# Token norms of a DeltaNet layer: squares by wide activations and sums by one-column matmuls in place of per-token accumulating activations

## The chip, the cores and the metric

The kernel runs on one core of one Trainium2 chip. The metric is device microseconds (us) of one execution. A core has TensorE (PE; the trace shows its weight loads apart, as PEld), VectorE (DVE), ScalarE (ACT), GpSimd (POOL) and SyncE (SP), whose queue here issues every DMA. Matmul results land in PSUM, which this kernel uses as eight banks, each a tile of 128 partitions by 512 words; the other tiles lie in SBUF.

## The reference, cut to what matters

One layer of a token mixer (a Fourier branch and a bidirectional gated DeltaNet branch) followed by a ConvFFN, for 1024 tokens and 256 context tokens of width 1024, in float32. The change touches three norms, each over the 128 channels of one head, per token:

```python
def l2norm(x):
    return x * lax.rsqrt(jnp.sum(x * x, axis=-1, keepdims=True) + L2_EPS)

qkv = jax.nn.silu(dwconv1d(p[..., OFF_Q:OFF_Z], conv_qkv)).astype(jnp.float32)
q, k, v = [a.reshape(b, t, DN_HEADS, DN_HEAD_DIM) for a in jnp.split(qkv, 3, axis=-1)]
q = l2norm(q) * (DN_HEAD_DIM ** -0.5)
k = l2norm(k)
...
o = (rms_norm(o_dn, dn_norm) * jax.nn.silu(zh)).astype(z.dtype).reshape(b, t, DN_WIDTH)
```

There are 8 heads. k is needed for 1280 tokens (1024 and the 256 of context), q and the delta output o for 1024. So the sums of squares are 8 x (10 + 8 + 8) = 208 blocks of 128 tokens by 128 channels.

## The kernel before, in words

**Layout.** A head's k, q, v and o stand with the 128 channels on the partitions and the tokens along the free axis (`xs` tiles of 128 x 1280, `qT` and `oo` of 128 x 1024). A norm per token is therefore a sum over partitions. The kernel wants it with the tokens on the partitions: one column of 128 values for each block of 128 tokens.

**How the order of the work is made.** `layer` (from line 488) only records operations. `Program.schedule` (line 351) is a list planner: it prices every operation with `cost` (line 247), takes the dependences from tiles and buffers, gives each operation a rank (the length of the priced path that hangs on it, plus a bonus) and builds one queue for each engine, which the engine then runs in order. PE is one such queue: a matmul that waits holds all that stand behind it. A PSUM bank counts as one whole in the dependences (line 305): a write to any part of it waits for the earlier reads of it by other engines. A buffer that several tiles share is handed on when the last user of the tile before is done (`gates`, line 323).

**The stages.** After the conditioning vector and the context projections, `project_kv` (line 942) makes k and v of a head: projection on PE with float32r matmuls in three terms (high and low halves), convolution taps on ACT and DVE, a SiLU (`silu_of_half`, line 754: tanh on ACT in pieces of 512 tokens into a tile of the ring `th`, which has two buffers, then one DVE operation), then ten blocks turned over by PE transposes in three groups (`o` in 8, 0, 4), copied out of PSUM by ACT (`tk`) and stored to `knd`. These transposes serve the stored token-major k and v; for k, ACT then squares each turned block in PSUM with an accumulating activation that leaves the 128 sums in one column of `ssq` (lines 965 to 967). Heads 0 to 3 take their banks from X0, X1, Y0, Y1, heads 4 to 7 from pm and pd in turn. `rk`, the inverse norm of k, is needed early: `coefs` (line 779) turns it into the factors of `decay_products`.

`kq_head` (line 1080) projects q and calls `query_norms`, which calls `squares` (line 762): eight transposes of `qT` in two groups of four into bank pd, eight accumulating squares. `scan_head` (line 1100) runs the recurrence over eight chunks in both directions, stores the output `oo`, and calls `squares` on it with the banks Y0 and Y1. Both results meet in `rs` (line 1126), the power on POOL, one small transpose and a store to `rsd`. `rsd` is read only in `gated` (line 1324), after all heads.

The main loop (line 1227) goes over ten stages (two context groups `c0`, `c1` and eight heads `x0` to `x7`): the scan of a stage, the block inversion (on DVE, with DMA round trips through DRAM) and merge of the next one, the q projection of the one after. `sides` fills in projections that nobody waits for soon (k and v of heads 4 to 7, the gates z and g). In the trace this delta part lies from about 100 to 1000 us. After it come the output projections, and from about 1300 us the ConvFFN.

**Prices that the planner uses** for the operations here: a transpose of 128 x 128 109 ns, a float32 matmul `n * 4 / 2.4 + 5` ns, where n is the larger of the columns of the moving and of the stationary operand (218 ns at 128, line 257), an activation `51 or 93 + 0.833 n` ns and 93 more with an accumulator (line 269).

Of the kernel before, what the change touches and what calls it, by code (L numbers as in the profile page):

```python
# [9 lines left out]
F32 = mybir.dt.float32  # L10
F32R = mybir.dt.float32r
AF = mybir.ActivationFunctionType
ALU = mybir.AluOpType
# [3 lines left out]
P = 128  # L17
# [8 lines left out]
EPS = 1e-6  # L26
AHEAD = 50
HALF = 512
# [160 lines left out]
class Program:  # L189
# [8 lines left out]
    def pool(self, name, bufs=1, space=None, side="left"):  # L198
        p = Pool(self, name, bufs, space, side)
        if space is None:  # L200
            self.events.append((True, p))
        return p
# [44 lines left out]
    def cost(self, eng, method, args, kw):  # L247
        out = args[0] if args else kw["out"]
        shape = out.shape
        n = math.prod(shape[1:])  # L250
        ins = [x for x in list(args[1:]) + list(kw.values()) if isinstance(x, View)]
        psum = any(v.slot.space == PSUM for v in ins)
        if eng == "PE":
            if method == "transpose":
                return max(53, args[1].shape[0] * 2 / 2.4 + 2)
            rhs, m = args[2], math.prod(args[1].shape[1:])
            n = max(math.prod(rhs.shape[1:]), m)
            if rhs.shape[0] <= 64 and m <= 64:
                return 34 if n <= 32 else 80
            return n / 2.4 + 3 if rhs.dtype == F32R and n >= 256 else n * 4 / 2.4 + 5  # L260
        if eng == "DVE":
            if method == "reciprocal":
                return 65 + 6.3 * n
            ptr = any(v.shape[-1] == 1 and v.arr.size <= P for v in ins) and method in ("tensor_scalar", "scalar_tensor_tensor")
            fast = method in ("tensor_copy", "tensor_scalar") and not psum and out.slot.space != PSUM
            return 66 + n / (1.92 if fast else 0.96) + (61 if ptr else 0)
        if eng == "ACT":
            aps = any(isinstance(kw.get(x), View) for x in ("scale", "bias", "accum_out"))
            return (51 if psum else 93) + n * 0.833 + (93 if aps else 0)
        if eng == "POOL":  # L270
            if method == "memset":
                return 36 + 0.83 * n
            if kw.get("op") == ALU.pow:
                return 300 + 165 * n
            if method == "tensor_copy":
                return 119 + 3.33 * n
            if method == "affine_select":
                return 1060
            return 140 + 2.12 * n
        run = 1  # L280
        view = out if isinstance(out, View) else args[1]
        if isinstance(view, View):
            a_ = view.arr
            for d in range(a_.ndim - 1, -1, -1):
                if a_.shape[d] > 1 and a_.strides[d] != run:
                    break
                run *= a_.shape[d]
        total = math.prod(shape) * 4
        return max(60.0, total / 359.0 * (1 if run * 4 >= 512 else 2))
# [192 lines left out]
def body(tc, a, out):  # L482
    prog = Program(tc)
    layer(prog, a, out)
    prog.run()


def layer(prog, a, out):
    te, ve, se, po, sp = (prog.eng[n] for n in ("PE", "DVE", "ACT", "POOL", "SP"))
    pool, close = prog.pool, prog.close  # L490

    const = pool("const", bufs=1)
# [4 lines left out]
    def cload(name, shape=None, src=None):  # L497
        src = a[name] if src is None else src
        t = const.tile(list(shape or src.shape), F32, name=f"c_{name}")
        sp.dma_start(t, src)  # L500
        return t

    def ps(tag, shape, name):
        return psum.tile(shape, F32, tag=tag, name=name, bufs=PPB if tag == "pp" else 1)
# [3 lines left out]
    def bank(shape, name):  # L508
        rota[1] += 1
        return ps(rota[0][rota[1] % len(rota[0])], shape, name)  # L510
# [4 lines left out]
    ident = cload("ident", src=a["cst"][:, 0:128])  # L515
# [3 lines left out]
    ones = const.tile([P, 2], F32, name="ones")  # L519
# [19 lines left out]
    def weights(src, name, eng=None, tags=("h", "l"), pl=None):  # L539
        return [halves(src[:, o:o + HALF], pl or wst, tags, f"{name}{o}", eng) for o in range(0, src.shape[-1], HALF)]  # L540

    def product(pt, wl, rhs, nk=KT):
        n = 0
        for k in range(nk):
            h, l = rhs(k)
            wh, wlo = wl[k // 4]
            ks = slice((k % 4) * P, (k % 4 + 1) * P)
            for w_, r_ in ((wh, h), (wh, l), (wlo, h)):
                te.matmul(pt, w_[:, ks], r_, start=n == 0, stop=n == 3 * nk - 1)
                n += 1  # L550

    def split(h, l, src, eng_h=None, eng_l=None):
        if eng_h is se:
            se.activation(h, src, AF.Copy)
        else:
# [7 lines left out]
    bufs = {"CL": 2, "xs": 2, "qT": 2, "kT": 2, "F": 4, "LT": 2, "th": 2,  # L563
            "N": 4, "qh": 2, "S": 4, "R": 2, "vt": 3}
# [4 lines left out]
    def dt(tag, name, shape=(P, T), dtype=F32):  # L569
        return dp.tile(list(shape), dtype, tag=tag, name=name, bufs=bufs.get(tag, 1))  # L570
# [4 lines left out]
    th = dt("vt", "tanh_c", (P, KT, 2))  # L575
# [48 lines left out]
    for k in range(KT):  # L624
# [4 lines left out]
        for half in range(1, 2):  # L629
            parts = halves(a["w_ada"][k * P:(k + 1) * P, half * 1024:(half + 1) * 1024], hx, ("H", "L"),  # L630
                           f"ada{k}{half}", (ve, po)[k % 2])
            for j in range(2):
                for i, w_ in enumerate(parts):
                    te.matmul(rows[half * 2 + j], s4[:, k, :], w_[:, j * HALF:(j + 1) * HALF], start=k + i == 0,
                              stop=k == KT - 1 and i == 1)
    prog.bonus = 0.0
    pm_ = ps("pm", [P, 16, 4], "modp")
    for q in range(4):
        n = (2, 4)[q // 2]
# [32 lines left out]
    NCH = 10  # L672
# [75 lines left out]
    def conv_taps(pt, acc, w3):  # L748
        n = acc.shape[-1]
        se.activation(acc, pt[:, 0:n], AF.Identity, scale=w3[:, 1:2])  # L750
        ve.scalar_tensor_tensor(acc[:, 1:n], pt[:, 0:n - 1], w3[:, 0:1], acc[:, 1:n], op0=ALU.mult, op1=ALU.add)
        ve.scalar_tensor_tensor(acc[:, 0:n - 1], pt[:, 1:n], w3[:, 2:3], acc[:, 0:n - 1], op0=ALU.mult, op1=ALU.add)

    def silu_of_half(acc, name):
        n = acc.shape[-1]
        for o in range(0, n, HALF):
# [2 lines left out]
            se.activation(th_, part, AF.Tanh)  # L759
            ve.scalar_tensor_tensor(part, th_, 1.0, part, op0=ALU.add, op1=ALU.mult)  # L760

    def squares(src, name, tags):
        ssq = const.tile([P, 8], F32, tag="ssq", name=f"ssq_{name}", bufs=3)
        for g in range(2):
            pt = ps(tags[g], [P, 4, P], f"sq_{name}{g}")
            for i in range(4):
                u = g * 4 + i
                te.transpose(pt[:, i, :], src[:, u * P:(u + 1) * P], ident)
            for i in range(4):
                se.activation(pt[:, i, :], pt[:, i, :], AF.Square, accum_out=ssq[:, g * 4 + i:g * 4 + i + 1])  # L770
        return ssq

    def query_norms(src, name):
        qn = const.tile([P, 8], F32, tag="qn", name=f"qn_{name}", bufs=3)
# [164 lines left out]
    rk_of = const.tile([P, NH, NCH], F32, name="rk_of")  # L939
    turn = [0]  # L940

    def project_kv(w, h):
        kv = "kv"[w]
        wl = weights((wi_k, wi_v)[w](h), f"{kv}{h}")
        dst = xsp.tile([P, T + TC], F32, tag="xs", name=f"xs{kv}{h}")
        w3 = convw[:, (w + 1) * 8 + h, :]
        pt = bank([P, HALF], f"pc{w}_{h}")
        product(pt[:, 0:TC], wl, hc)
        conv_taps(pt, dst[:, T:T + TC], w3)
        proj_taps(wl, dst, w3, f"x{kv}_{h}")  # L950
        silu_of_half(dst, f"th{kv}{h}")
        if w == 0:
            sp.dma_start(kvd[h], dst)
            ssq = const.tile([P, NCH], F32, tag="ssq", name=f"ssq_k{h}", bufs=3)
        for o in (8, 0, 4):
            n = min(4, NCH - o)
            turn[0] += 1
            tags = XY if h < 4 else ("pm", "pd")
            pt = ps(tags[turn[0] % len(tags)], [P, 4, P], f"tt{kv}{h}_{o}")
            for i in range(n):  # L960
                te.transpose(pt[:, i, :], dst[:, (o + i) * P:(o + i + 1) * P], ident)
            tk = dp.tile([P, 4, P], F32, tag="tk", name=f"tk{kv}{h}_{o}", bufs=2)
            se.activation(tk[:, 0:n, :], pt[:, 0:n, :], AF.Copy)
            sp.dma_start(knd[w, h, :, o:o + n, :], tk[:, 0:n, :])
            if w == 0:
                for i in range(n):
                    se.activation(pt[:, i, :], pt[:, i, :], AF.Square, accum_out=ssq[:, o + i:o + i + 1])
        if w == 0:
            rk = rk_of[:, h, :]
            ve.tensor_scalar(rk, ssq, EPS, None, op0=ALU.add)  # L970
            po.tensor_tensor(rk, rk, mhalf[:, 0:NCH], op=ALU.pow)

    def load_tokens(w, name, src):
# [242 lines left out]
    for h in range(4):  # L1216
        project_kv(0, h)
# [36 lines left out]
    for g4 in range(NF):  # L1254
# [18 lines left out]
        for e in range(2):  # L1273
            pt = ps(("pd", "pm")[e], [P, 4, P], f"dft{g4}{e}")
            for i in range(4):
                te.matmul(pt[:, i, :], quad[:, e, i // 2, (i % 2) * P:(i % 2 + 1) * P], csd[:, e * P:(e + 1) * P],
                          start=True, stop=True)
            se.activation(gh[:, e], pt, AF.Copy)
        pt = ps("pd", [1, P], f"mid{g4}")
# [4 lines left out]
        for e in (1, 0):  # L1284
            pt = ps(("pm", "pd")[e], [P, 2, QT], f"dfp{g4}{e}")
            for odd in range(2):
                more = e == 0 and odd == 0
                for i in range(2):
                    te.matmul(pt[:, odd, :], gh[:, e, odd * 2 + i, :], waves[e][:, odd, i, :], start=i == 0,
                              stop=i == 1 and not more)  # L1290
# [12 lines left out]
    pt = ps("pd", [P, NF], "dftn")  # L1303
# [196 lines left out]
    for ts in ((0,), (1,), (2,), (3,), (4,), (5, 6, 7)):  # L1500
# [20 lines left out]
        g = ts[-1] // 4  # L1521
        prog.bonus = BON * (1 - g)
        for k in (0, 4, 1, 5, 2, 6, 3, 7) if g == 0 else (4, 5, 6, 7, 0, 1, 2, 3):
            pt = transposed(xn[-4:], k, f"h2{g}", ("pd", "pm")[k % 2])
# [273 lines left out]
```

## Time and profile before

| | |
|---|---|
| runs | 2049.98, 2051.59, 2053.32 us, median 2051.59 |
| profiled execution | 2047.95 us, of which the span of the program's instructions is 2046.2 us |
| granted TensorE clock, mean | 0.979 |
| PE busy | 1953.0 us (95%), 11470 instructions |
| weight loads (PEld) | 1570.9 us (77%) |
| DVE / ACT / POOL busy | 1363.1 / 858.1 / 564.0 us |
| ACT squares with accumulator, blocks of 128 x 128 in PSUM | 208, each followed by a readout of the accumulator |

How to read it: a group's row gives the operation, the shapes (stationary operand as rows*columns for PE, then the moving or source tile), the count, then the busy time in us, the mean of one in ns, and the idle time of the engine before them with what ended it. A timeline row gives start and length in us of a run of like instructions, their count, and in brackets the idle time before the first. PE and PEld records overlap each other; the pitch (start to start) and not the mean length is what one more instruction costs. All instructions carry line 349, the place where the recorded operations are issued, so the names of tiles (p for PSUM, m for SBUF, d for DRAM) and the shapes tell them apart.

### The profile page before, as it was taken

How to read it: one execution, taken by the hardware profiler on the slowest of the kernel's cores; microseconds unless marked ns; L12 is line 12 of the kernel's file. 1: busy time of each engine (PE TensorE's matmuls, PEld its weight loads, DVE VectorE, ACT ScalarE, POOL GpSimd, SP SyncE). 2: the span in 40 equal slices, each digit the busy share in tenths (PEclk: the TensorE clock that was granted, in tenths of full speed). 3: DMA queues.
4: the chain of work that ended last, by engine and by line, in shares of the span. 5: the costliest groups of instructions: out<-in, count | busy, mean ns of one | idle time of the engine just before them, and what ended most of it. 6: DMA issues, size and time to landing. Idle time of an engine off the chain costs nothing.

```text
span 2046.2 us, 31495 instructions
## 1 busy us (share of the span) xinstructions
PE 1953.0 (95%) x11470; PEld 1570.9 (77%) x11470; DVE 1363.1 (67%) x2848; ACT 858.1 (42%) x2088; POOL 564.0 (28%) x573
## 2 busy tenths in 40 slices
PE   8989999899999999999999999979999999999998
PEld 3868888787777788778776778857878888878886
DVE  5648767667677577673655485479988889882132
ACT  5575354555354453632431032454444444532121
POOL 3110121101112220210221000257878888600000
PEclk9989999899999999999999999999999999999999
DMA  7153324344451543441778562312222222453231
GB/s 298 52 187 92 105 88 132 117 145 128 113 149 52 149 150 92 118 114 51 223 234 289 181 221 102 114 52 78 95 75 80 83 83 86 167 181 100 77 126 52
DMA packets 180637, 257.52 MB, mean 126 GB/s; under 512 B 75921, under 2 KB 97522, under 8 KB 180482
## 3 DMA queue, kind: packets, MB, share of 16 engines
q1 hardware_dynamic: 180482, 255.51, 39.0%
q8 instruction: 90, 1.47, 0.3%
q14 instruction: 65, 0.53, 0.1%
HBM read 194.52 MB, written 60.94 MB: 125 GB/s over the span
## 4 chain that ended last, share of the span: by engine, by line
PE 71%; DVE 14%; DMA 5%; ACT 5%; issue 2%; POOL 1%; SPq 0%; DVEq 0%; POOLq 0%; ACTq 0%
PE p L349 71%; DVE m L349 11%; ACT m L349 4%; DMA m<-d 3%; DVE p L349 3%; DMA d<-m 2%; ACT p L349 1%; POOL m L349 1%; DMA m<-in_w_ada_dram 1%; SPq L349 0%; DMA m<-in_wu_dram 0%; ACT L349 0%; DVEq L1787 0%; POOLq L1787 0%; DVEq L349 0%
## 5 line engine op out<-in xcount | busy, mean ns | idle before, releaser
L349 PE MATMUL p<-m,m 128*128 128x512 f32 (+7 forms) x11310 | 1937.8, 338 | 75.7 <-ACT m L349 31.6
L349 PEld LDWEIGHTS p<-m,m 128*128 128x128 f32 (+4 forms) x11310 | 1551.2, 174 | 452.6 <-ACT m L349 62.4
L349 DVE TENSOR_TENSOR m<-m,m 128x512 fp32r<-128x512 f32 (+27 forms) x1096 | 557.4, 523 | 253.4 <-ACT m L349 222.8
L349 ACT ACTIVATE m<-m 128x512 fp32r<-128x512 f32 (+8 forms) x649 | 411.3, 652 | 613.5 <-DMA m<-d 161.0
L349 POOL TENSOR_TENSOR m<-m,m 128x512 fp32r<-128x512 f32 (+5 forms) x338 | 449.5, 1353 | 782.6 <-DVE m L349 625.1
L349 ACT ACTIVATE m<-p 128x512 f32<-128x512 f32 (+5 forms) x510 | 221.1, 448 | 329.3 <-PE p L349 286.0
L349 DVE SCALAR_TENSOR_TENSOR m<-p,m,m 128x128 f32<-128x128 f32 (+4 forms) x488 | 203.1, 452 | 92.3 <-ACT m L349 40.9
L349 DVE SCALAR_TENSOR_TENSOR p<-m,m,p 128x512 f32<-128x512 f32 x352 | 240.1, 749 | 2.7 <-ACT p L349 0.4
L349 ACT ACTIVATE m<-p,m 128x128 f32<-128x128 f32 (+2 forms) x240 | 115.7, 495 | 184.3 <-PE p L349 179.5
L349 POOL MEMSET m<- 128x1024 f32 (+7 forms) x79 | 35.7, 460 | 381.7 <-PE p L349 224.0
L349 POOL COPY m<-m 32x256 f32<-32x256 f32 (+2 forms) x136 | 60.3, 447 | 211.5 <-DMA m<-d 173.7
L349 DVE SCALAR_TENSOR_TENSOR m<-m,m 128x512 f32<-128x512 f32 (+5 forms) x119 | 65.7, 558 | 28.6 <-ACT m L349 16.3
L349 DVE COPY m<-p 32x256 f32<-32x256 f32 (+11 forms) x116 | 42.1, 368 | 62.5 <-PE p L349 32.8
L349 DVE TENSOR_TENSOR m<-p,m 128x512 f32<-128x512 f32 (+4 forms) x91 | 57.8, 645 | 30.5 <-PE p L349 29.1
L349 DVE SCALAR_TENSOR_TENSOR m<-m,m,m 128x1024 f32<-128x1024 f32 (+2 forms) x68 | 59.6, 878 | 26.0 <-DMA m<-in_w_ada_dram 25.6
L349 DVE TENSOR_TENSOR m<-m,p 128x128 f32<-128x128 f32 (+3 forms) x117 | 53.4, 458 | 29.6 <-PE p L349 28.8
L349 ACT ACTIVATE p<-p 128x128 f32<-128x128 f32 x208 | 55.4, 266 | 25.6 <-PE p L349 23.6
L349 DVE SCALAR_TENSOR_TENSOR m<-m,p 128x512 f32<-128x512 f32 x76 | 50.7, 682 | 13.9 <-ACT m L349 7.7
L349 DVE SCALAR_TENSOR_TENSOR m<-m,m,p 128x128 f32<-128x128 f32 x128 | 42.7, 342 | 23.5 <-PE p L349 22.8
L349 ACT ACTIVATE m<-m,m 128x128 f32<-128x128 f32 (+1 forms) x168 | 54.6, 406 | 6.3 <-DMA m<-d 3.6
L349 POOL TENSOR_SCALAR_AFFINE_SELECT m<-m 128x1024 f32<-128x1024 f32 x16 | 18.9, 1199 | 100.4 <-DVE m L349 100.4
L349 DVE SCALAR_TENSOR_TENSOR m<-m 128x1 f32<-128x1 f32 (+1 forms) x25 | 4.7, 188 | 54.3 <-ACT m L349 54.2
(20 smaller groups left out, 210.3 us busy)
## 6 DMA issues: line engine op xcount, KB each, us to landing
m<-d SPq DMA_DIRECT2D x76, 512.0 KB
d<-m SPq DMA_DIRECT2D x138, 256.0 KB
m<-d SPq DMA_DIRECT2D x114, 256.0 KB
m<-in_wi_dram SPq DMA_DIRECT2D x106, 256.0 KB
m<-in_w_ada_dram SPq DMA_DIRECT2D x48, 512.0 KB
m<-in_wu_dram SPq DMA_DIRECT2D x88, 256.0 KB
m<-in_wn_dram SPq DMA_DIRECT2D x26, 512.0 KB
m<-d SPq DMA_DIRECT2D x44, 192.0 KB
```

Source lines behind the costliest of these rows:

```text
L349: return getattr(engine.real, method)(*[real(v) for v in args], **{k_: real(v) for k_, v in kw.items()})
```

## The change

The transposes and accumulating squares are replaced. `token_sums` squares the channel-major tile in pieces of up to 512 tokens with one activation from SBUF to a tile of the `th` ring, and then, for each block of 128 tokens, makes the squared block the stationary operand of a float32 matmul with a single column of ones, so that the 128 sums land in one PSUM column. For q and o the eight transposes go away; they use one bank (the first of the two names). For k the transposes stay, since `knd` is stored from them; the ten sums go into unused columns of the bank of the first group (`o == 8`), which is kept until `rk` has been read from it. The planner gets a price for a float32 matmul with a one-column moving operand: 0.9 ns for each stationary column, 115 ns at 128.

```diff
@@ cost
             rhs, m = args[2], math.prod(args[1].shape[1:])
+            if rhs.dtype != F32R and math.prod(rhs.shape[1:]) == 1:
+                return max(60, m * 0.9)
             n = max(math.prod(rhs.shape[1:]), m)
@@ layer
+    def token_sums(src, pt, name):
+        n = src.shape[-1]
+        for o in range(0, n, HALF):
+            part = src[:, o:min(o + HALF, n)]
+            sq_ = dt("th", f"sq_{name}_{o}", part.shape)
+            se.activation(sq_, part, AF.Square)
+            for i in range(part.shape[-1] // P):
+                u = o // P + i
+                te.matmul(pt[:, u:u + 1], sq_[:, i * P:(i + 1) * P], ones[:, 0:1], start=True, stop=True)
+
     def squares(src, name, tags):
-        ssq = const.tile([P, 8], F32, tag="ssq", name=f"ssq_{name}", bufs=3)
-        for g in range(2):
-            pt = ps(tags[g], [P, 4, P], f"sq_{name}{g}")
-            for i in range(4):
-                u = g * 4 + i
-                te.transpose(pt[:, i, :], src[:, u * P:(u + 1) * P], ident)
-            for i in range(4):
-                se.activation(pt[:, i, :], pt[:, i, :], AF.Square, accum_out=ssq[:, g * 4 + i:g * 4 + i + 1])
-        return ssq
+        pt = ps(tags[0], [P, 16], f"sq_{name}")
+        token_sums(src, pt, name)
+        return pt[:, 0:src.shape[-1] // P]
@@ project_kv
         if w == 0:
             sp.dma_start(kvd[h], dst)
-            ssq = const.tile([P, NCH], F32, tag="ssq", name=f"ssq_k{h}", bufs=3)
         for o in (8, 0, 4):
...
             sp.dma_start(knd[w, h, :, o:o + n, :], tk[:, 0:n, :])
-            if w == 0:
-                for i in range(n):
-                    se.activation(pt[:, i, :], pt[:, i, :], AF.Square, accum_out=ssq[:, o + i:o + i + 1])
+            if w == 0 and o == 8:
+                ssq = pt[:, 2, 0:NCH]
+                token_sums(dst, ssq, f"k{h}")
+                rk = rk_of[:, h, :]
+                ve.tensor_scalar(rk, ssq, EPS, None, op0=ALU.add)
         if w == 0:
-            rk = rk_of[:, h, :]
-            ve.tensor_scalar(rk, ssq, EPS, None, op0=ALU.add)
             po.tensor_tensor(rk, rk, mhalf[:, 0:NCH], op=ALU.pow)
```

## The prediction

> **What bounds the kernel now.** First the page: span, busy times, and the chain of work that ended last.
>
> ```profile
> span 2046.2 us, 31495 instructions
> PE 1953.0 (95%) x11470; PEld 1570.9 (77%) x11470; DVE 1363.1 (67%) x2848; ACT 858.1 (42%) x2088; POOL 564.0 (28%) x573
> PE 71%; DVE 14%; DMA 5%; ACT 5%; issue 2%; POOL 1%; SPq 0%; DVEq 0%; POOLq 0%; ACTq 0%
> ```
>
> PE is busy for 95% of the span and carries 71% of the chain; ACT is at 42% and 5%. Work taken from ACT is worth something only where PE stands and waits for it; work added to PE is worth its own length unless it falls into time in which PE stood still. Next, busy time by stretch (PE, PEld, DVE, ACT, POOL, granted clock, DMA share, GB/s) and what PE waited for in the delta part alone, where all of the change lies.
>
> ```profile
> 100.00:400.00 300.00, 277.60 (x2129) 233.19 (x2127) 206.57 (x566) 167.34 (x518) 48.95 (x81) 0.96 0.40 121
> 400.00:700.00 300.00, 279.40 (x2320) 227.92 (x2321) 211.14 (x632) 144.27 (x438) 47.16 (x85) 0.95 0.42 122
> 700.00:1000.00 300.00, 294.23 (x2252) 244.66 (x2250) 197.20 (x556) 131.93 (x402) 48.37 (x74) 0.99 0.39 114
> PE p L349 <- ACT m L349: 15.5, 11, 4.2
> PE p L349 <- DMA m<-d: 14.3, 7, 8.7
> PE p L349 <- DVE m L349: 14.2, 22, 2.3
> PE p L349 <- ACT p L349: 1.8, 2, 1.0
> by line: PE p L349 64.0%; DVE m L349 16.1%; DMA m<-d 6.6%; ACT m L349 5.4%; DMA d<-m 3.3%; issue 2.6%; ACT p L349 1.5%; SPq L349 0.3%; POOL m L349 0.1%; DVEq L349 0.0%; ACTq L349 0.0%; POOLq L349 0.0%
> ```
>
> From 100 to 1000 us PE is busy 277.60 + 279.40 + 294.23 = 851.2 of 900 us, so it idles 48.8 us. That is all that added PE work could hide in. The last row is the chain in that stretch: writes of ACT to PSUM, which here are the squares, hold 1.5% of 900 us, 13.5 us. That is all that a faster ACT norm could take off the chain directly.
>
> **Part 1, the matmuls with one column of ones (PE, added).** There are 8 x (10 + 8 + 8) = 208. First, how many passes is each? Two rows by form:
>
> ```profile
> L349 PE MATMUL p<-m 128*128 128x128 f32 x160 | 25.5, 296 | 9.8 <-DMA m<-d 9.2 <-DVE m L349 0.5
> L349 PE MATMUL p<-m,m 128*8 128x128 f32 x8 | 2.6, 321 | 0.0
> ```
>
> The first are the products of k with itself, 8 for each of ten stages, 80 in the code: 160 records, so a float32 matmul goes through PE twice. The second are the 8 small transposes of `rs`, one for each head: 8 records, so a transpose goes through once. A one-column matmul is float32, hence two passes, and each needs its own load of a 128 x 128 stationary block. No one-column matmul with 128 x 128 weights stands in this trace; the nearest is the one with four columns, at the end of the Fourier part, then its two passes and the next loads:
>
> ```profile
> 1006.79 0.19 PEld L349 LDWEIGHTS p<-m,m 128*128 128x128 f32 x1 [0.33 <-ACT m L349]
> 1006.79 0.52 PEld L349 LDWEIGHTS p<-m,m 128*128 128x128 f32 x4 [0.33 <-ACT m L349]
> 1006.79 0.39 PE L349 MATMUL p<-m,m 128*128 128x4 f32 x2
> 120.43 2.44 PE L349 MATMUL p<-m,m 128*128 128x512 f32 x13
> L349 PE MATMUL p<-m,m 128*128 128x512 f32 x7 | 2.4, 428 | 0.0
> L349 PE MATMUL p<-m,m 128*128 128x80 f32 x6 | 1.0, 253 | 0.0
> 116.77 2.45 PE L349 MATMUL p<-m,m 128*128 128x512 f32 x10
> L349 PE MATMUL p<-m,m 128*128 128x512 f32 x6408 | 1622.4, 403 | 41.2 <-ACT m L349 25.6 <-DVE m L349 13.1 <-ACT p L349 1.0
> ```
>
> One load takes 0.19 us from start to end, four take 0.52, so the pitch of a load is (0.52 - 0.19) / 3 = 0.11 us although only four columns stream. Two passes are 0.22 us. Would a wide matmul in between hide a load? The lower rows answer that: thirteen records near 120 us, seven of 512 columns and six of 80 (three float32 matmuls set singly between the wide ones), take 2.44 us. Ten wide ones alone take 2.45 with a mean record of 0.40, a pitch of (2.45 - 0.40) / 9 = 0.228. In the mixed row the six wide ones after the first take 6 x 0.228 = 1.37 of 2.44 - 0.40 = 2.04, and 0.67 is left for three narrow float32 matmuls: 0.22 each. So the load does not vanish between wide neighbours. I take 0.222: 208 x 0.222 = +46.2 us of PE. The lower bound is one pass of 0.11, +22.9; the upper bound the 0.23 of a wide pitch, +47.8. The planner's new price of 115 ns lies at the lower bound and is no measurement of this trace.
>
> The Trainium skill, "TensorE: Matmul & The Clock Gate", section "Part 2: What happens when you issue a matmul", would have it otherwise: the queue pulls weight loads ahead of running matmuls, so the next tile's weights load while this one streams. If that covered both loads, the 208 matmuls would cost nearly nothing and the sum below would turn into a gain. The trace agrees for wide matmuls only (their pitch of 0.228 holds a load) and not for the narrow ones beside them.
>
> **Part 2, the transposes of q and o (PE, removed).** Their number is 8 x 16 = 128. Those of k stay, since the stored tokens are made from them.
>
> ```profile
> 466.22 0.60 PE L349 MATMUL p<-m,m 128*128 128x128 f32 x4
> L349 PE MATMUL p<-m,m 128*128 128x128 f32 x4 | 0.6, 273 | 0.0
> ```
>
> Four transposes take 0.60 us with a record of 0.27 each, so the pitch is (0.60 - 0.27) / 3 = 0.11: 128 x 0.109 = -14.0 us. PE alone: +46.2 - 14.0 = +32.2 us. By head it is 10 x 0.222 = 2.2 us for k and 0.9 each for q and o.
>
> **Part 3, the squares (ACT).** Removed are 208 accumulating squares of 128 x 128; added are 8 x (2 + 2 + 2) = 48 squares of 512 columns and 8 of 256.
>
> ```profile
> L349 ACT ACTIVATE p<-p 128x128 f32<-128x128 f32 x208 | 55.4, 266 | 25.6 <-PE p L349 23.6
> L349 ACT ACTIVATION_READ_ACCUMULATOR p<-p 128x1 f32 x208 | 40.1, 193 | 0.0
> 128.37 0.29 ACT L349 ACTIVATE p<-p 128x128 f32<-128x128 f32 x1
> 128.66 0.28 ACT L349 ACTIVATE p<-p 128x128 f32<-128x128 f32 x1
> 99.26 1.15 ACT L349 ACTIVATE m<-m 128x512 f32<-128x512 f32 x2
> L349 ACT ACTIVATE m<-m 128x512 f32<-128x512 f32 x80 | 50.0, 629 | 51.0 <-DVE m L349 30.7 <-DMA m<-d 13.7 <-issue 6.4
> L349 ACT ACTIVATE m<-m 128x256 f32<-128x256 f32 x16 | 6.7, 418 | 1.5 <-DVE m L349 1.5
> ```
>
> Square and readout overlap; their pitch is 128.66 - 128.37 = 0.285 us, 59.3 us in all. A wide one costs 1.15 - 0.63 = 0.52 when it follows another, and one of 256 columns 0.31 (0.52 less the difference of the mean records, 0.629 - 0.418): 48 x 0.52 + 8 x 0.31 = 27.4. ACT is relieved by some 32 us, but at 49% busy in this part (167.34 + 144.27 + 131.93 of 900) most of it hides behind PE. What it is worth is read where PE waited:
>
> ```profile
> 464.72 0.26 ACT L349 ACTIVATE p<-p 128x128 f32<-128x128 f32 x1 [2.09 <-PE p L349]
> 470.54 4.50 ACT L349 ACTIVATE m<-m,m 128x128 f32<-128x128 f32 x15
> 478.33 1.22 PE L349 MATMUL p<-m,m 128*128 128x512 f32 x2 [3.47 <-ACT m L349]
> 673.96 0.26 ACT L349 ACTIVATE p<-p 128x128 f32<-128x128 f32 x1
> 681.74 1.85 PE L349 MATMUL p<-m,m 128*128 128x512 f32 x4 [2.47 <-ACT m L349]
> 612.38 1.22 PE L349 MATMUL p<-m,m 128*128 128x512 f32 x2 [4.18 <-ACT m L349]
> ```
>
> At 478.33 PE had waited 3.47 us for an eviction that stood on ACT behind the decay exponentials, which stood behind the batch of squares that begins at 464.72, 15 until 470.5: 15 x 0.285 = 4.3 less the wide ones in their place, some 1.1, so up to 3.2 us go. At 681.74 a batch of five ending with the one at 673.96, and one more, stand in the same place, 6 x 0.285 = 1.7. At 612.38 no square is near, and nothing goes. With the 1.8 us that PE waited for banks held by squares that is 6.7; the chain says 13.5 x (1 - 27.4 / 59.3) = 7.3. I take -6, bounds -8 and 0.
>
> **Part 4, what the idle time absorbs.** Added matmuls cost nothing where PE would have stood still soon after, for something that does not wait for them. Such stalls are 8.74 us before 147.25 (a DMA round trip; only the last head's 2.2 us of sums lie ahead of it), a string of waits of a stage's inversion and merge from 383 to 402 (the largest 2.26) and the stretch after 608 with the 4.18 above and more such pieces. Of the 32.2 us I let these take 7, about half of 8.74 + 2.26 + 4.18 = 15.2; bounds 0 and that 15.2.
>
> ```profile
> 147.25 2.08 PE L349 MATMUL p<-m 128*128 128x128 f32 x8 [8.74 <-DMA m<-d]
> 392.04 1.97 PE L349 MATMUL p<-m,m 64*64 64x64 f32 x32 [2.26 <-DVE m L349]
> ```
>
> **Part 5, new waits.** The sums stand in PE's ordered queue and now wait for a square that ACT makes; behind them stand the projections of the next head. The `th` ring's next tanh waits until PE has used the square before. For heads 4 to 7 one of two banks (pm, pd) is kept from the first transpose until `rk` is read, so the third group of the same head, the decay products (pd) and the merges (pm) queue up behind ten matmuls. All this is paid only where the planner's slots don't cover it, and the planner puts each sum at 115 ns where the rows say 222. I take +3; lower bound 0, upper bound 24 groups x 0.63 (one wide square each) + 4 heads x 2.2 = +24. The reads of the sums from PSUM in place of SBUF are 24 DVE instructions of 8 or 10 columns; no DMA is added, and `rs` is read only after 1000 us, so these go at nothing (0.1 us each, 2 us, if they were all on the path).
>
> **Sum.** +46.2 - 14.0 - 6 - 7 + 3 = +22 us on the profiled 2047.95, which is 2070. The profiled execution lies below all three runs (2049.98 to 2053.32), so I put the same difference on their median: 2051.59 + 22 = 2073.6. The forecast's own range, the terms moved half of the way to their bounds together, with the passes left at 0.222, is 2067 (-1 on ACT, -4 on absorption, -1.5 on waits) to 2091 (+3, +3.5, +10.5).
>
> **The rivals.** (a) *Half price.* If each one-column matmul takes one load of 0.11, as the planner's price says, PE gains 22.9 - 14.0 = +9; with -6 from ACT and -3 absorbed the time is 2051.59, no change. For it speaks only that four columns are not one; against it the 0.11 pitch, which did not depend on the columns. (b) *Not slower: the delta part is bound by its chain and not by PE.* The chain there has only 64.0% PE, the rest being DVE, DMA and ACT steps of the stages. If every added matmul falls into the 48.8 us of idle time and the squares leave the chain, the gain is 7.3 us: 2044. The place is the stretch from 100 to 1000 us; it decides if PE's idle time there ends near 48.8 - 32.2 - 7.3 = 9 us. Against it: the fillers keep PE at 98% from 700 on, and the stalls stand where DMA returns, not where sums would be. (c) *New waits at full price*: +24 in place of +3, 2051.59 + 43 = 2095; it shows as PE's wait for ACT rising from 15.5 us to over 30 in that stretch.
>
> **Chances.** Forecast 0.68, (a) 0.10, (b) 0.10, (c) 0.12. The range reaches from just below (a) to the edge of (c), 2049 to 2094; it leaves out (b) and half of (c). A difference within 0.2% (4.1 us) can't be told from none. Faster: (b) and a little of (a), 0.11. Same: half of (a) and the mildest end of the forecast, 0.09. Slower 0.80.
>
> **What the changed profile would show.** Right: 416 records of one column on PE and 416 loads, at a pitch of 0.11; PE's busy time in the delta part up by about 32 us; ACT's busy time there down; the readouts of accumulators in PSUM gone; the parts after 1000 us of the same length, only later. Wrong: a pitch near 0.06 (then (a)); the same start of the output projections with fuller PE (then (b)); a long wait for ACT or PSUM in front of the sums (then (c)). The largest single risk is part 4, since a new order of the planner moves all stalls at once.

## The result and the profile after

The changed kernel is slower: median 2064.28 us of 12 runs (2058.16 to 2072.4) against 2052.34 us of the kernel before in the same comparison (12 runs, 2048.66 to 2060.44). The ratio is 1.0054, 95% interval 1.0036 to 1.0072, so +11.1 us (7.4 to 14.8). The forecast was +22 us with a range from 2049 to 2094: the direction and the range held, the size forecast was twice what came.

The profiled execution took 2065.40 us, a span of 2063.7. It lies 17.5 us above the profiled one before; the medians differ by 12, because the profiled execution of before lies below its median. First the page of the changed kernel, with the chain by engine:

```profile
span 2063.7 us, 31710 instructions
PE 1991.1 (96%) x11758; PEld 1605.5 (78%) x11758; DVE 1367.8 (66%) x2848; ACT 827.8 (40%) x1728; POOL 565.4 (27%) x573
PE 79%; DVE 9%; DMA 4%; ACT 3%; issue 2%; POOL 1%; SPq 0%; DVEq 0%; POOLq 0%; ACTq 0%
```

PE's busy time rose by 38.1 us, ACT's fell by 30.3, PE has 288 records more (416 one-column passes for 128 transposes), and the chain went from 71% to 79% PE. Next the delta part of the changed kernel by stretch (PE, PEld, DVE, ACT, POOL, granted clock, DMA share, GB/s), what PE waited for there, and the chain there:

```profile
100.00:400.00 300.00, 293.08 (x2163) 249.66 (x2165) 204.72 (x560) 149.07 (x332) 45.73 (x74) 0.98 0.40 121
400.00:700.00 300.00, 283.80 (x2321) 232.97 (x2308) 206.49 (x623) 136.30 (x341) 45.11 (x80) 0.98 0.42 123
700.00:1000.00 300.00, 293.99 (x2449) 244.42 (x2450) 190.87 (x544) 120.64 (x310) 43.23 (x80) 0.99 0.35 102
PE p L351 <- ACT m L351: 14.6, 20, 2.3
PE p L351 <- DVE m L351: 10.5, 16, 3.1
PE p L351 <- DMA m<-d: 0.6, 1, 0.6
by line: PE p L351 75.2%; DVE m L351 9.6%; ACT m L351 4.3%; DMA d<-m 4.3%; DMA m<-d 2.9%; issue 1.9%; DMA m<-in_wi_dram 1.0%; SPq L351 0.7%; POOL m L351 0.1%; ACTq L351 0.0%; DVEq L351 0.0%; POOLq L351 0.0%
```

From 100 to 1000 us PE is busy 870.9 us and idles 29.1, where it had idled 48.8. The waits for a DMA, 14.3 us before, are nearly gone; the waits for ACT stayed (15.5 to 14.6). The new work has its own rows, and the loads their pitch: two loads from 96.91 on end after 0.31 us, seven after 0.87.

```profile
L351 PE MATMUL p<-m,m 128*128 128x1 f32 x416 | 53.4, 238 | 2.1 <-ACT m L351 1.9
L351 ACT ACTIVATE m<-m 128x512 f32<-128x512 f32 x128 | 78.4, 627 | 86.8 <-DVE m L351 43.4 <-DMA m<-d 18.7 <-PE p L351 18.1
96.91 0.31 PEld L351 LDWEIGHTS p<-m,m 128*128 128x128 f32 x2
96.91 0.87 PEld L351 LDWEIGHTS p<-m,m 128*128 128x128 f32 x7
```

That is (0.87 - 0.31) / 5 = 0.112 us for each one-column pass: the price of part 1, measured. The delta part of both kernels as a whole, up to the start of the last Fourier steps (975 us before, 992 after):

```profile
97.00:975.00 878.00, 829.77 (x6598) 690.48 (x6597) 596.16 (x1716) 435.82 (x1343) 135.00 (x232) 0.97 0.39 117
```

```profile
97.00:992.00 895.00, 865.97 (x6900) 724.62 (x6898) 596.64 (x1713) 404.74 (x981) 131.65 (x230) 0.98 0.39 115
```

PE is busy 36.2 us more and idles 19.2 us less (48.2 to 29.0); what comes after this part is as long as before, 1071 us in both. So the loss is made wholly here, and the question is why 36 us of PE work cost 11 to 17. One thing in these two rows matters later: the granted clock is 0.97 before and 0.98 after.

### The profile page after: what moved, and what is told of

It reads as the page before. It is cut to its first block, busy times and chain, and to the rows that moved or that the text cites. A ratio compares the mean times of both kernels' runs of the same rounds, so it can differ in the third digit from the quotient of the medians.

```text
span 2063.7 us, 31710 instructions
## 1 busy us (share of the span) xinstructions
PE 1991.1 (96%) x11758; PEld 1605.5 (78%) x11758; DVE 1367.8 (66%) x2848; ACT 827.8 (40%) x1728; POOL 565.4 (27%) x573
## 4 chain that ended last, share of the span: by engine, by line
PE 79%; DVE 9%; DMA 4%; ACT 3%; issue 2%; POOL 1%; SPq 0%; DVEq 0%; POOLq 0%; ACTq 0%
PE p L351 79%; DVE m L351 8%; ACT m L351 3%; DMA d<-m 2%; DVE p L351 2%; DMA m<-d 1%; POOL m L351 1%; DMA m<-in_wi_dram 0%; SPq L351 0%; DVEq L1792 0%; POOLq L1792 0%; ACTq L351 0%; DVEq L351 0%; POOLq L351 0%
## 5 line engine op out<-in xcount | busy, mean ns | idle before, releaser
L351 PE MATMUL p<-m,m 128*128 128x512 f32 (+6 forms) x11598 | 1978.4, 336 | 64.6 <-ACT m L351 29.7
L351 PEld LDWEIGHTS p<-m,m 128*128 128x128 f32 (+3 forms) x11598 | 1587.1, 174 | 446.2 <-ACT m L351 66.9
L351 DVE TENSOR_TENSOR m<-m,m 128x512 fp32r<-128x512 f32 (+25 forms) x1096 | 558.7, 523 | 243.4 <-ACT m L351 219.0
L351 ACT ACTIVATE m<-m 128x512 fp32r<-128x512 f32 (+9 forms) x705 | 441.9, 647 | 668.4 <-DMA m<-d 167.4
L351 ACT ACTIVATE p<-m,m 128x512 f32<-128x512 f32 x44 | 30.2, 691 | 20.5 <-DVE m L351 20.1
```

Of the source, the lines that this page charges most:

```text
L351: return getattr(engine.real, method)(*[real(v) for v in args], **{k_: real(v) for k_, v in kw.items()})
```

## The experiments

All ratios are to the kernel before, taken on the same chip. Where a run is said to keep the order, the queue of every engine holds the same operations in the same order as the kernel named. Beside the edit itself there is only one DVE operation that makes a tile of ones in runs E, F, G and L, and run J issues the pieces of a square in a row. A distance from the changed kernel is the difference of the two ratios times 2052 us.

**A. The planner's price put back.** The two lines of `cost` that were added are taken out again.

```diff
-            if rhs.dtype != F32R and math.prod(rhs.shape[1:]) == 1:
-                return max(60, m * 0.9)
```

> The changed kernel with the planner's price of a one-column matmul left as it was before (218 ns, close to the 222 ns of the trace, in place of 115). Only the order of the work can differ. If the loss of 11 us comes from PE work itself, the time stays within 4 us of the changed kernel's 2064. If it comes from an order made with a wrong price, it falls back to 2056 or less.

Measured 1.0042 (1.0029 to 1.0056), median 2058.42 us. The intervals of both kernels overlap, and the difference of 2.5 us is below what can be told. The wrong price is not where the loss is.

**B and C. Half of the change each.** B keeps the old `squares` for q and o (first diff); C keeps the old block of `project_kv` (second diff).

```diff
-        token_sums(src, pt, name)
+                te.transpose(pt[:, i, :], src[:, u * P:(u + 1) * P], ident)
...
+                se.activation(pt[:, i, :], pt[:, i, :], AF.Square, accum_out=ssq[:, g * 4 + i:g * 4 + i + 1])
```

```diff
-                token_sums(dst, ssq, f"k{h}")
...
+                    se.activation(pt[:, i, :], pt[:, i, :], AF.Square, accum_out=ssq[:, o + i:o + i + 1])
```

> Only the sums of k are new; q and o keep transposes and accumulating squares. PE work against before is 80 x 0.222 = +17.8 us, ACT -(80 x 0.285 - 24 x 0.45) = -12. If the loss follows PE work (11 of 32 us passed on), it is about +6 us, 2058. If the loss sits in k alone (early sums in front of the projections, a bank kept), it is the whole +11, 2063.

> Only the sums of q and o are new; k is as before. PE work against before is 128 x (0.222 - 0.109) = +14.4 us, ACT -(128 x 0.285 - 32 x 0.52) = -20. If the loss follows PE work it is about +5 us, 2057; if it sits in k alone, 2050 to 2054 or, by the relief of ACT, somewhat faster than before.

Measured: k alone 1.0083 (1.0060 to 1.0105), median 2067.78 us; q and o alone 1.0049 (1.0030 to 1.0068), median 2059.52 us. The halves together should cost +27 us; the whole costs 11. Neither expectation covers k alone being slower than the whole. A sum of parts fails here. Each part is planned anew, and run K below prices that; besides, the mean granted clock of the executions is 0.981 in both halves, 0.980 before and 0.987 with the whole change.

**D. Each sum twice.**

```diff
-                te.matmul(pt[:, u:u + 1], sq_[:, i * P:(i + 1) * P], ones[:, 0:1], start=True, stop=True)
+                for _ in range(2):
+                    te.matmul(pt[:, u:u + 1], sq_[:, i * P:(i + 1) * P], ones[:, 0:1], start=True, stop=True)
```

> The changed kernel with each one-column matmul issued twice: 208 more, +46.2 us of PE at 0.222 and nothing else. If PE work in this part is passed on in full, 2064 + 46 = 2110. If idle time goes on absorbing half or more of it, 2075 to 2087. If the loss was the order and not the work, within 6 us of 2064.

Measured 1.0394 (1.0372 to 1.0416), median 2128.72 us: (1.0394 - 1.0054) x 2052 = 70 us above the changed kernel for 46 us of work, more than passing it on in full. Its delta part shows why the work is not all:

```profile
97.00:1052.00 955.00, 932.62 (x7297) 794.87 (x7297) 597.62 (x1712) 404.44 (x980) 130.27 (x229) 0.95 0.36 108
497.00:504.00 7.00, 7.00 (x51) 6.52 (x52) 6.18 (x21) 2.88 (x6) 1.40 (x2) 1.00 0.94 319
504.00:511.00 7.00, 7.00 (x41) 6.19 (x40) 3.35 (x12) 6.76 (x20) 1.77 (x1) 0.75 0.68 256
511.00:514.00 3.00, 3.00 (x13) 2.67 (x12) 2.69 (x11) 1.44 (x3) 0.00 (x0) 0.50 0.02 5
L351 PE MATMUL p<-m,m 128*128 128x1 f32 x32 | 3.6, 247 | 0.0
```

PE has no idle time from 497 to 514 us, yet the granted clock falls from 504 on: to a mean of 0.75 in seven microseconds and of 0.50 in the three after them. In the seven microseconds ahead of that, 32 of 51 records are one-column passes (last row). A clock of 0.95 in the delta part, where the changed kernel has 0.98, is some 28 us over 932.62 us of busy PE, an estimate from these rows; with the 46 us of work that covers the 70.

**E. The sums in one pass, same order.** Squares and ones as float32r, which PE takes in one pass (two columns of ones; the squares are thereby rounded to float32r).

```diff
-            sq_ = dt("th", f"sq_{name}_{o}", part.shape)
+            sq_ = dt("th", f"sq_{name}_{o}", part.shape, F32R)
-                te.matmul(pt[:, u:u + 1], sq_[:, i * P:(i + 1) * P], ones[:, 0:1], start=True, stop=True)
+                te.matmul(pt[:, 2 * u:2 * u + 2], sq_[:, i * P:(i + 1) * P], ones_r[:, 0:2], start=True, stop=True)
```

> The changed kernel with the squares written as float32r and the sums taken by one float32r pass (against two columns of ones) in place of two float32 passes; every engine's queue keeps the order of the changed kernel. PE loses 208 passes of 0.111, -23 us. If PE work in this part is passed on in full, 2064 - 23 = 2041, faster than before. If only the third that the whole change showed (11 of 32) is passed on, 2056. If the order is what costs, within 4 us of 2064.

Measured 0.9961 (0.9945 to 0.9976), median 2043.30 us: 19 us (14 to 24) below the changed kernel, for 208 passes, 23 us, less. It is faster than before by 0.4%.

```profile
97.00:977.50 880.50, 839.80 (x6682) 699.49 (x6681) 592.91 (x1711) 403.39 (x980) 130.60 (x230) 0.98 0.39 116
L351 PE MATMUL p<-m,m 128*128 128x2 f32 x208 | 29.6, 222 | 2.6 <-ACT m L351 2.4 <-DVE m L351 0.2
```

PE is busy 26.2 us less than in the changed kernel and still 10.0 us more than before, and yet the time is below before. What makes up for the 10.0 us, the order, the lighter ACT or a granted clock of 0.98 in place of 0.97, this run alone doesn't tell.

**F and G. One pass, in the halves.** G is E with q and o only (the order of C), F is E with k only (the order of B).

> The float32r sums for q and o only, k as before. PE work equals that of the kernel before (128 passes of 0.111 in place of 128 transposes of 0.109), ACT is relieved of 128 x 0.285 - 32 x 0.52 = 20 us. What remains is the relief of ACT and the new order: 2044 to 2050 if the relief counts, 2048 to 2054 if it is hidden.

> The float32r sums for k only; q and o as before. PE against before is 80 x 0.111 = +9 us, ACT -12. By work alone +3 to +8 us, 2054 to 2059. If q and o are what cost (their run alone at equal PE work was 11 us slower), it is faster than 2050.

Measured: q and o 1.0053 (1.0035 to 1.0071), median 2062.57 us, so 128 passes fewer than C (14 us) changed nothing, 1.0049 to 1.0053. k 0.9952 (0.9939 to 0.9966), median 2042.57 us, so 80 passes fewer than B (9 us) brought 27 us, 1.0083 to 0.9952. What a pass costs seems to depend on where it stands. The same operation in kernels of one order tells where: the second pair of triangle masks on POOL, near 350 to 390 us, when k of all heads is made, and the last mask (the second number of the lower row, the last start). For the changed kernel and E:

```profile
385.71 2.67 POOL L351 TENSOR_SCALAR_AFFINE_SELECT m<-m 128x1024 f32<-128x1024 f32 x2 [5.67 <-DVE m L351]
L351 POOL TENSOR_SCALAR_AFFINE_SELECT m<-m x16: 1081/1092/1635, 261.5 to 926.5; 128x1024 f32<-128x1024 f32 x16
```

```profile
372.09 2.67 POOL L351 TENSOR_SCALAR_AFFINE_SELECT m<-m 128x1024 f32<-128x1024 f32 x2 [5.92 <-DVE m L351]
L351 POOL TENSOR_SCALAR_AFFINE_SELECT m<-m x16: 1081/1092/2324, 253.0 to 913.9; 128x1024 f32<-128x1024 f32 x16
```

E is 13.6 us ahead at the first and 12.6 at the last: all of its gain in this part is made before 390 us. In the same rows of the other pairs, F is ahead of B by 14.3 and 18.2, G of C by -0.6 and 0.6. The sums of k, made while PE is the bound, are paid; halving the sums of q and o, nearly all later, brought nothing that the time shows.

**H. A light stand-in, same order.** Only the first sum of each square is a full one, the rest load one column; most norms then come from another block of tokens.

```diff
+                if i == 0:
+                    te.matmul(pt[:, u:u + nb], sq_[:, 0:P], ones[:, 0:nb], start=True, stop=True)
+                else:
+                    te.matmul(pt[0:1, u:u + 1], sq_[:, i * P:i * P + 1], ones[:, 0:1], start=True, stop=True)
```

> The order and all waits of the changed kernel, but only one full sum for each square (56); the other 152 matmuls load one column in place of 128 and write one row, so most norms come from another block of tokens. PE loses some 152 x (0.222 - 0.06) = 25 us, by an estimated 0.03 for each narrow pass. Passed on in full: 2039; a third: 2056. What is left over before at 2052, less the 14 us of transposes, is the worth of the relief of ACT.

Measured 1.0006 (0.9991 to 1.0021), median 2051.91 us, 10 us below the changed kernel. PE's busy time in the delta part fell by 16 us (865.97 to 849.9), not by 25, so the estimate of 0.03 for a light pass was too low; some 60% was passed on.

**I. A wide stand-in, same order.** Each sum is taken against 256 columns, so no pass is narrow; all columns of a norm hold the sums of the last block.

```diff
+    onesw = ones[:, 0:1].broadcast_to([P, 256])
+                te.matmul(pt, sq_[:, i * P:(i + 1) * P], onesw, start=True, stop=True)
```

> The order and all waits of the changed kernel, but each sum is taken against 256 columns of ones (a broadcast), so that a pass streams 0.21 to 0.23 us in place of 0.111, and all columns of a norm hold the sums of the last block. PE gains 208 x (0.44 - 0.222) = +45 us, as in the run with each sum issued twice, but no pass is narrow. If the 64 us of that run came partly from a clock halved by narrow passes, this one stays at 2064 + 45 = 2109 or less with a granted clock of 0.98 or more; if not, it is near 2128 too.

Measured 1.0216 (1.0195 to 1.0237), median 2095.44 us: 33 us above the changed kernel for 33 us more busy time of PE (899.36 against 865.97), and

```profile
97.00:1020.00 923.00, 899.36 (x6894) 749.26 (x6893) 595.79 (x1711) 404.55 (x980) 134.51 (x230) 0.99 0.38 112
```

a granted clock of 0.99 in the delta part, against 0.95 with each sum issued twice. As much extra work was meant in both; the narrow one costs 70, the wide one 33. The two orders differ, so not all of the gap need be the clock.

**J. The ACT work put back, same order.** Each wide square is issued as squares of 128 columns with an accumulator whose column nobody reads.

```diff
+                parts = [(o.args, o.kw)]
...
+                    parts = [((t_[:, j:j + P], src[:, j:j + P], o.args[2]), {"accum_out": self.spare[:, (self.spent + j // P) % 52:(self.spent + j // P) % 52 + 1]})
+                             for j in range(0, t_.shape[-1], P)]
...
+                for more in parts[1:]:
+                    q = self.issue(self.eng[o.eng], o.method, *more).ins
```

> The changed kernel in the same order of every queue, but each wide square is issued as squares of 128 columns with an accumulator (its column is never read), so that ACT has its 208 squares and readouts back, some 32 us or a little more, and PE is unchanged. If the relief of ACT is worth the 6 us of the prediction, 2070; if it is worth the 16 us that seem to be missing beside the PE work, 2080; if those came from the new order, within 3 us of 2064.

Measured 1.0114 (1.0085 to 1.0144), median 2074.88 us: 12 us (5 to 19) above the changed kernel.

```profile
97.00:1011.00 914.00, 885.29 (x6901) 737.52 (x6901) 596.82 (x1714) 435.31 (x1328) 131.39 (x230) 0.97 0.37 112
388.26 2.68 POOL L351 TENSOR_SCALAR_AFFINE_SELECT m<-m 128x1024 f32<-128x1024 f32 x2 [5.66 <-DVE m L351]
L351 POOL TENSOR_SCALAR_AFFINE_SELECT m<-m x16: 1083/1094/1637, 261.1 to 943.2; 128x1024 f32<-128x1024 f32 x16
```

ACT is at 435.31 us, what it was before the change (435.82). The masks show where the time grew: 2.6 us behind the changed kernel at the second pair, 16.7 at the last (this execution is 18 us longer than the profiled changed one). But PE does not wait more for ACT. It idles 914.00 - 885.29 = 28.7 us in the delta part, against 29.0 in the changed kernel; its waits for ACT (first row below) are 15.6 us against 14.6, and no wait for a DMA came back. What grew is PE's busy time, by 19.3 us for the same instructions, at a granted clock of 0.97 in place of 0.98. The second row is one of the stretches in which the clock stood at a half:

```profile
PE p L351 <- ACT m L351: 15.6, 25, 2.1
482.20:492.40 10.20, 10.20 (x39) 9.04 (x38) 6.29 (x21) 8.52 (x35) 1.37 (x1) 0.50 0.52 197
```

So with the work back on ACT the time is longer, but by a lower clock of PE and not by waits for ACT. Why the clock falls more often then was not tested.

**K and L. Another order alone.** K is the kernel before with one constant of the planner changed, L is E with the planner's price of a sum at 218 ns.

```diff
-MIX = 0.1
+MIX = 0.11
```

> The kernel before with one constant of the planner moved from 0.10 to 0.11 (how much the recorded order weighs in a rank), the same instructions in another order. It measures what another order alone does: within 0.2% of before if the order hardly matters, 0.4% or more to either side if the differences of the runs with parts of the change are of that kind.

> The kernel with float32r sums, planned with a price of 218 ns for a sum in place of 115: the same instructions in another order. If its gain over before (0.4%) comes from the work, 2040 to 2047; if it comes from a lucky order, 2050 or more.

Measured: K 0.9940 (0.9920 to 0.9960), median 2042.66 us. The same instructions in another order are 12 us faster than before, as much as the whole change lost. L 0.9960 (0.9946 to 0.9974), median 2044.05 us, the same as E: its gain does not hang on one lucky order of its own.

## Why the prediction was right, and where its size was off

**Part 1, the pitch of a sum, was right.** Two passes, 0.112 us each, taken from a matmul with four columns. Rival (a) fell with it, and run E shows what it would have been: with one pass for each sum the kernel is 0.4% faster than before, where (a) had said no change.

**Part 2 and the balance on PE look right in size**: +32.2 us predicted, 36.2 measured in the delta part. But the 36.2 were measured at a better clock, and by the estimate of the next paragraph the added work is nearer 44 us at one clock. Where the other 12 us come from was not traced.

**The granted clock: a term that the prediction lacks, and the likeliest reason for its size.** Part 4 took a filled stall to be worth its own idle time and no more. The traces show a second worth: after a stall PE ran at half the clock. First two rows of the kernel before, at the stall of 8.74 us ahead of 147.25, then the wide matmuls right behind it:

```profile
138.50:142.60 4.10, 0.01 (x1) 0.00 (x0) 0.00 (x0) 3.16 (x13) 0.00 (x0) 1.00 0.96 321
142.70:156.30 13.60, 8.53 (x27) 6.97 (x28) 6.68 (x24) 13.59 (x39) 2.45 (x3) 0.50 0.47 155
149.13 2.90 PE L349 MATMUL p<-m,m 128*128 128x512 f32 x6
L349 PE MATMUL p<-m,m 128*128 128x512 f32 x11 | 5.3, 643 | 0.0
```

Six wide matmuls take 2.90 us there with a mean record of 0.64, a pitch of (2.90 - 0.64) / 5 = 0.45 us, twice the 0.228 of part 1. The next rows add up all the stretches of the delta part in which the clock stood at a half, for the kernel before (six), the changed one (five) and run J (twelve): their length, then the busy time of PE and the other engines in them.

```profile
sum 57.80, PE 39.19 PEld 29.83 DVE 31.79 ACT 36.01 POOL 18.59; mean PE 6.53 PEld 4.97 DVE 5.30 ACT 6.00 POOL 3.10
sum 27.20, PE 24.14 PEld 19.42 DVE 10.85 ACT 12.01 POOL 9.44; mean PE 4.83 PEld 3.88 DVE 2.17 ACT 2.40 POOL 1.89
sum 57.80, PE 56.99 PEld 47.14 DVE 31.12 ACT 33.45 POOL 17.17; mean PE 4.75 PEld 3.93 DVE 2.59 ACT 2.79 POOL 1.43
```

If half of PE's busy time in them is lost, that is 19.6 us before, 12.1 after and 28.5 in run J. By this estimate the change got back 7.5 us through the clock, and run J lost 16.4 of the 18 us by which its profiled execution is longer than that of the changed kernel. The single executions say the same. At a mean granted clock of 0.984, the three of the kernel before (in the comparisons of the experiments) took 2045.24, 2046.38 and 2046.74 us and the two of the changed kernel 2069.73 and 2071.67, some 24 us apart. The medians are only 12 apart, at clocks of 0.980 and 0.987 on average. So the 22 us of the forecast are near what the change costs at one clock, and the forecast had no term for the part that the clock gave back. No run holds the clock fixed, so this is an account from traces, not a test.

**Part 3, the worth of the lighter ACT, stays open.** ACT's work fell by 31.1 us (435.82 to 404.74), as predicted (some 32). Its worth was put at 6 us, with a bound of 8. Run J, in the same order, gives 12 (5 to 19), in which the 6 lies, and most of what its trace shows is the clock. Executions with like clocks, run J at 0.987 and 0.989 (2073.1, 2063.13) and the changed kernel there (2064.92 at 0.987, 2058.16 and 2059.09 at 0.989), are 4 to 8 us apart. PE's waits for a DMA (14.3 to 0.6 us) do not hang on ACT's load: none came back in run J. They stayed at 12.5 with the new sums for q and o only and fell to 4.3 with those for k only.

**Part 4, the absorbed work, fits run E as a total and was wrong as a picture.** E against the changed kernel, both at a mean clock of 0.987, passes on 19 (14 to 24) of 23 us, so some 17% is absorbed; the prediction let 7 of 32.2 go, 22%. But it is not a share of every sum. Before 390 us E gains 13.6 us where its halved sums, the 80 of k and those of the first q, are about 10 us of passes; after it, nothing. Here too the clock has a share: after 390 us PE is busy at half the clock for 25.45 us in E and 13.94 in the changed kernel, some 6 of the 11.5 us that E's later passes save. The stalls that the prediction named as covers, 383 to 402 and after 608, do lie where the free sums of q and o are.

**Part 5 and the rest.** In the profiled executions PE's work rose by some 44 us at one clock (predicted 32.2), its idle time fell by 19.2 (predicted 6 + 7 - 3 = 10, for ACT, absorption and new waits together) and the clock gave back 7.5 (no term): 17 us in all. The first two deviations, +12 and -9, nearly cancel, which is luck, and the third is most of what keeps the sum below 22; the medians lie closer still, 11.1 us apart (7.4 to 14.8). How the 19.2 us divide among ACT, absorption and new waits, put at +3, is open. No run shows the new waits by themselves, and run K says that another order alone moves this kernel by 12 us, so they can't be told from the luck of the order. The prediction named that as its largest risk but gave it no price.

**The rivals.** (b) asked that PE's idle time in the delta part end near 9 us; it ended at 29.1, and the time rose. (c) asked that its wait for ACT rise over 30 us; it is 14.6. What is left open: why each half alone (+17 and +10) costs as much as the whole or more. The halves have orders of their own, and K shows that this is enough to do it; their granted clock is also lower than that of the whole (0.981 against 0.987). Which of the two it is was not shown.

## What to carry to other kernels

Price a narrow matmul by its weight load and its number of passes, not by its columns; in one float32r pass the sums that lost 0.5% gain 0.4%. Work moved between engines is to be priced in each stretch of the kernel: where PE was the bound, its sums were paid in full, and in the later stages halving them brought nothing that the time shows. Look at the granted clock beside the busy times before a gain is put down to a relieved engine: here a filled stall was worth its idle time and, in this trace, half of the matmul time behind it that ran at half the clock. Where a planner orders the work, measure another order of the same instructions before a difference of half a per cent is put down to a change. Of all kernels run, the old one in another order (0.9940) and the one with float32r sums for k only (0.9952) are the quickest, and their intervals overlap.

## What the runs showed of the hardware

The granted clock falls after idle time of PE: each of the six stretches at a half in the delta part of the kernel before begins after PE idled 1.9 to 4.1 of the 6.8 us ahead of it. But it also falls where PE is never idle, behind many narrow passes. In the changed kernel this happens once, from 331.3 to 334.7 us, with PE busy throughout:

```profile
324.00:331.00 7.00, 7.00 (x42) 5.96 (x41) 2.23 (x4) 2.01 (x4) 0.00 (x0) 1.00 0.20 56
331.30:334.70 3.40, 3.40 (x17) 3.31 (x16) 1.05 (x3) 2.33 (x6) 1.95 (x1) 0.50 0.24 77
L351 PE MATMUL p<-m,m 128*128 128x1 f32 x20 | 2.6, 225 | 0.0
```

Twenty of the passes ahead of the drop have one column. With k alone there are three such drops of 3.4 us (at 134.7, 145.0 and 274.7), each with 20 one-column passes and no idle time in the 6.8 us ahead. Where the sums take one pass, run F has no drop before 390 us, and the two of run E (at 142.3 and 295.9) stand behind 2.4 and 1.6 us of idle time. In run B, at half the clock, the three drops cost 5 us, and with the 9 us of passes saved they make up the 14.3 us of run F at the second pair of masks. So a narrow pass may cost more than its 0.112; that the passes themselves bring the clock down is argued from where they stand, and from run I, whose wide passes in the same places kept 0.99. The Trainium skill, "TensorE: Matmul & The Clock Gate", section "What's actually happening", lets the clock fall after a window of about 3.4 us in which PE is idle. The traces agree on the window (drops last 3.4 us or a multiple) and, in the kernel before, on idle time ahead, but not on idleness as the profile shows it in the changed kernel: here the busy time was 7.00 of 7.00 us.
